# Writing down VectorE's order in an expert stream, with gathered rows used one block later

## The chip, the cores and the metric

One core of a Trainium2 chip runs the whole program. The metric is the device time of one execution in microseconds (us); the median of three runs of the kernel before is 4095.1 us (4092.52 to 4101.62). The engines are TensorE (PE in the profile; PEld is its weight load), VectorE (DVE), ScalarE (ACT), GpSimd (POOL) and SyncE (SP, which here only issues transfers).

## The reference

Two transformer blocks run one after the other on 512 tokens of width 1024. Each ends in a layer of 16384 single-row experts, which is the part that matters here:

```python
def block(xb):                                  # 128 tokens
    q = (xb @ w_q).reshape(PEER_BLOCK, PEER_HEADS, 2, PEER_QDIM // 2)
    s = jnp.einsum('thsd,hsnd->thsn', q, sub_keys)
    sv, si = lax.top_k(s, PEER_TOPK)            # 16 of 128 keys, twice, for 8 heads
    ...
    e = jnp.take_along_axis(cidx, pos, axis=-1) # 128 experts for each token
    g = jax.nn.softmax(top, axis=-1)
    act = jax.nn.gelu(jnp.einsum('thkd,td->thk', u_tab[e], xb), approximate=False)
    w = (g * act).astype(xb.dtype)
    return jnp.einsum('thk,thkd->td', w, v_tab[e])
```

Everything is float32. The kernel splits a float32 operand into a high half (rounded to TensorE's fp32r) and a low half (the rest), and takes three products: high by high, low by high, high by low.

## The kernel before

The program has two expert streams, one for each block of the network: about 960 to 1960 us and 3105 to 4085 us of the profile. Both are made by the function `peer`. Of the 512 tokens, 384 (three tiles) are *dense*: all 16384 experts are computed for them, 128 at a time, with gates that are zero where an expert was not picked. The fourth tile is *gathered*: for each of its 128 tokens the 128 picked rows of both tables are fetched by indirect transfers.

The stream's loop runs over e = 0 to 127, blocks of 128 experts. The names below are those of the profile.

- **A(e)**, `emit_A`, runs NA = 28 blocks ahead: `ur` is loaded (SP), `uh` is its high half (ScalarE), `ul` its low half (GpSimd, L1105), 24 products give `pa` (TensorE, L1112 to L1115), and ScalarE makes `ga`, the gelu of it.
- **Block e itself**: `vr` is loaded, `vh` is its high half (ScalarE, L1262), `vl` its low half (L1263; VectorE, but in the first stream GpSimd for e = 100 to 119). `w` is gate times `ga` (VectorE, L1267), `wh` and `wl` its halves (ScalarE L1268, VectorE L1269). 18 products, y(e), add them up over all 128 blocks (TensorE, L1293 to L1295). The tiles w, wh, wl, vh and vl have two buffers each, so wh(e), wl(e), vh(e) and vl(e) can be written only when y(e-2) has been read.
- **Gathered rows**: 128 events of kind u (`urow`: fetch the row k of every token, L1229; multiply by the token's input and sum into `act[:, k]`, L1230) and 128 of kind v (`vrow`: fetch, L1241; add `act` times the row to `acc`, L1243). After each 16 u there is a gelu on ScalarE (L1233) and a product with the gates on VectorE (L1234). The list `ev` has u alone first, then u and v in turn, then v alone; it is spread over blocks 2 to 100, some 2.6 rows in a block. The tiles `urow` and `vrow` have three buffers each.

Two things set the order. On TensorE, VectorE, ScalarE and SP, a planner that runs when the program is built takes the instruction that comes first in the program among those whose inputs it reckons ready. On GpSimd, within `manual_schedule`, the order is that of the program. After that each engine executes its own list strictly in order. In the list that the planner made for VectorE, w is two blocks ahead of its use, and the row instructions stand between vl, wl and w.

In the first stream a side job, `modulation` (L823, L825), runs on VectorE from e = 100.

Of the kernel before, what the change touches and what calls it, by code (L numbers as in the profile page):

```python
# [8 lines left out]
F32 = mybir.dt.float32  # L9
# [4 lines left out]
AF = mybir.ActivationFunctionType  # L14
OP = mybir.AluOpType
# [8 lines left out]
def build(tc, I, out, dbg=None, stop=None):  # L24
# [28 lines left out]
    def rsqrt(ssq, n, scale, nm, eps=EPS):  # L53
        """1 / sqrt(ssq * scale + eps) for a [128, n] tile."""
# [24 lines left out]
    def transpose_split(src, ncol, hi, lo, dst, psum=None):  # L79
        """src [128, ncol*128] -> hi/lo[:, k, dst] for each 128-column chunk k."""  # L80
        for k0 in range(0, ncol, 4):
            n = min(4, ncol - k0)
            pool, tag = psum or (pst, "tr")
            pt = pool.tile([128, 4, 128], F32, name="pt", tag=tag)
            for k in range(n):
                T.transpose(pt[:, k, :], src[:, (k0 + k) * 128:(k0 + k + 1) * 128], ident)
            split(dst_view(pt[:, 0:n, :], dst, src=True), dst_view(hi[:, k0:k0 + n, :], dst), dst_view(lo[:, k0:k0 + n, :], dst))
# [6 lines left out]
    def ssq_of(src, junk, nm):  # L94
        """sum of squares along the free axis on the scalar engine"""
        s = sm.tile([src.shape[0], 1], F32, name=nm, tag="ssq")
        A.activation(out=junk, in_=src, func=AF.Square, accum_out=s)
        return s
# [6 lines left out]
    def load_w(W, k, c0, cn, pool=None, e=V):  # L105
        """rows of chunk k of a weight matrix, as high and low halves"""
# [23 lines left out]
    def proj(hiT, loT, W, K, c0, cn, evac, tiles=range(NT), pool=None):  # L130
        """token-major product: for each token tile, psum[128, cn] = h @ W[:, c0:c0+cn]"""
# [16 lines left out]
    def keep_w(pool, W, K, c0, cn=512, last=0, e=V):  # L148
        """a block of weight columns on chip, for products of one token tile after the other"""
        room = [pool.tile([128, 2, 512], F32R, name=f"wk{i}") for i in range(K)]  # L150
        return [load_w(W, k, c0, cn, room[(k + K - last) % K], e) for k in range(K)]
# [10 lines left out]
    def proj_rows(hiT, loT, ws, evac, then):  # L162
        """all token tiles in turn; then(t) follows two tiles behind"""
# [7 lines left out]
    # token order of everything after the first mixing: row p of tile r is token 4 p + r  # L171
# [6 lines left out]
    # =====================================================================  # L178
    # block 1: norm, input projection
    # =====================================================================  # L180
# [43 lines left out]
    def head_proj(pool, hi, lo, W, c0, nh, hd, tiles, finish, first=None, wait=False):  # L224
        """nh heads of width hd divided by their root mean square; finish(t, heads, scale)"""
# [92 lines left out]
    def cmul(o_r, o_i, a_r, a_i, b_r, b_i, pool, shape, conj_b=False, e=V):  # L318
        """o = a * b (or a * conj b)"""
# [22 lines left out]
    # powers a^0 .. a^8  # L342
# [14 lines left out]
    # c a^n: real part and negated imaginary part  # L357
# [16 lines left out]
    # unit phases e^{i Theta j}, Theta = 8 theta, and the decay of a chunk  # L374
# [37 lines left out]
    def coefficients():  # L412
        s5x = ExitStack()
        s5t = s5x.enter_context(tc.tile_pool(name="s5t", bufs=1, side="right"))
        # chunk-input coefficients, transposed to [(s, c), pair, (g2, p)]
# [12 lines left out]
        # block-Toeplitz matrices [(s, c_in), g, (t, c_out)], two groups of a pair at a time  # L428
# [94 lines left out]
    def norm_T(xt, gain, hi, lo, sl, pool, inplace=False, two=False):  # L523
        """rmsnorm of a [128, 1024] tile with gain, transposed and split"""
# [218 lines left out]
    def softmax_row(ps, n, z, pool, tag="pe"):  # L743
        """exp(scores - max) with its sum"""
# [43 lines left out]
    def modulation(rows, pool, psum, tags, ptag, on_pool):  # L788
        """rows of the modulation; yields after each block of 128 x 1024 weights"""
# [57 lines left out]
    EV = 100  # L847
# [6 lines left out]
    def queries(qp, Wq, hi, lo):  # L854
        """loads, halves and products of the 128-column blocks of the query weights"""
# [31 lines left out]
    def peer_route(rw, query, keysT, crep, E, GT, ahead, also, first):  # L887
        """expert indices (as float) and gates, [128, tile, 128 slots]

        Step l of 16 is one half of one head's query; the candidates of a head are  # L890
        looked up in the steps of the next head, and products of the first expert
        blocks run between the steps' products."""
# [23 lines left out]
        def top16(src, work, vals, idx, tiles):  # L916
            """the 16 largest of src[:, t] with their places, in order"""
# [96 lines left out]
        def more(e):  # L1014
            """product e, then the halves of block e + 2, whose room it frees"""
# [39 lines left out]
    RG = (3, 6, 9, 11)  # L1055

    def peer_front(nm, Wq):
        """room for the transposed input, and for its making"""
# [11 lines left out]
    def peer(keysT_d, U, UT, Vt, front, finish, nm, side=None, also=None, then=None):  # L1070
# [86 lines left out]
        # slot-major indices and gates of the dense tokens  # L1157
        # first index = 16 a + b; rows a, b, second index (bf16 holds them) and gate
# [68 lines left out]
        def g_u(k):  # L1227
            row = gw.tile([128, 1024], F32, name="urow", tag="row")
            G.indirect_dma_start(out=row, out_offset=None, in_=U, in_offset=bass.IndirectOffsetOnAxis(ap=ei[:, TL, k:k + 1], axis=0))  # L1229
            V.scalar_tensor_tensor(out=row, in0=row, scalar=1.0, in1=hg_, op0=OP.mult, op1=OP.mult, accum_out=act[:, k:k + 1])  # L1230

        def g_w(k0):
            A.activation(out=act[:, k0:k0 + 16], in_=act[:, k0:k0 + 16], func=AF.Gelu)  # L1233
            V.tensor_tensor(out=act[:, k0:k0 + 16], in0=act[:, k0:k0 + 16], in1=GT[:, TL, k0:k0 + 16], op=OP.mult)  # L1234

        vrow = {}

        def g_v(k):
            if k < 128:
                vrow[k] = gw.tile([128, 1024], F32, name="vrow", tag="vrow")  # L1240
                G.indirect_dma_start(out=vrow[k], out_offset=None, in_=Vt, in_offset=bass.IndirectOffsetOnAxis(ap=ei[:, TL, k:k + 1], axis=0))  # L1241
            if k >= 2:
                V.scalar_tensor_tensor(out=acc, in0=vrow.pop(k - 2), scalar=act[:, k - 2:k - 1], in1=acc, op0=OP.mult, op1=OP.add)  # L1243

        ev = []
        for k in range(128 + 34):
            if k < 128:
                ev.append((g_u, k))
                if k % 16 == 15:
                    ev.append((g_w, k - 15))  # L1250
            if k >= 32:
                ev.append((g_v, k - 32))

        pend = []
        for e in range(128):
# [6 lines left out]
            A.copy(out=vh, in_=vr)  # L1262
            (G if side and EV <= e < EW else V).tensor_tensor(out=vl, in0=vr, in1=vh.bitcast(F32), op=OP.subtract)  # L1263
# [3 lines left out]
            V.tensor_tensor(out=w.rearrange("p (a b) -> p a b", b=TG), in0=gbuf[:, :, e % EB, :], in1=gas.pop(e).rearrange("p (a b) -> p a b", b=TG), op=OP.mult)  # L1267
            A.copy(out=wh, in_=w)  # L1268
            V.tensor_tensor(out=wl, in0=w, in1=wh.bitcast(F32), op=OP.subtract)  # L1269
            with tc.manual_schedule(engines={mybir.EngineType.Pool}):  # L1270
                if e + NA < 128:
                    emit_A(e + NA)
                want = min(len(ev), max(0, (len(ev) * (e + 1 - GS) + GE - 1) // GE))
                while nev < want:
                    f_, k_ = ev[nev]
                    f_(k_)
                    nev += 1
# [47 lines left out]
    def fin1(t, acc, pool, psum):  # L1325
        """sum, then the first normalization of the second block"""
# [30 lines left out]
    def first_rows():  # L1357
        """the second block's first projection, by token tiles"""
# [12 lines left out]
    # lambda of the differential attention, on every partition  # L1371
# [48 lines left out]
    # =====================================================================  # L1420
    # block 2
    # =====================================================================
# [23 lines left out]
    def rope_proj(which, dst, c0, nh, col, first=None):  # L1446
        """projection, head norm, rotation and transposition of nh heads, from 128-column chunk c0 of dst on"""
# [77 lines left out]
    # the residual waits in memory while its room holds the values  # L1525
# [52 lines left out]
    def projT(hi, lo, W, K, c0, evac, n=4):  # L1578
        """feature-major product: for each 128-column chunk, psum[128, tokens] = W[:, chunk].T @ h"""
# [190 lines left out]
def sincos(nc, pool, ang, shape, c, s):  # L1770
    """cosine and sine of any angle: reduced by whole turns in three exact steps"""
# [20 lines left out]
def host_arrays(a):  # L1792
    """layout only"""
# [73 lines left out]
```

## Time and profile before

| | |
|---|---|
| median of three runs | 4095.1 us (4092.52 to 4101.62) |
| profiled execution, first to last instruction | 4090.4 us |
| TensorE busy (weight load) | 3876.8 us, 95% (3370.2 us, 82%) |
| VectorE busy | 3004.6 us, 73% |
| ScalarE busy | 1654.8 us, 40% |
| GpSimd busy | 2145.8 us, 52% |
| bytes moved | 784.31 MB, mean 192 GB/s |
| mean granted TensorE clock | 0.975 of full speed |

The profile is of one execution, whose own time is known only as its span of 4090.4 us; what lies outside the first and the last instruction is the 4.7 us to the median. An engine's busy time leaves out its waits, which the views below put down to what ended them. A matmul's end is modelled, so starts of matmuls are the safe figures.

### The profile page before, as it was taken

Reading aid. Unit: us, or ns where it says so; the run is one execution under the profiler, and the core shown is the slowest. Engines: PE = TensorE matmul, PEld = TensorE weight load, DVE = VectorE, ACT = ScalarE, POOL = GpSimd, SP = SyncE. Lnnn points to the kernel's source line nnn. Section 1 sums busy time; section 2 is a strip of 40 time slices with the busy share of each in tenths; the row PEclk is TensorE's granted clock in tenths of the full one; section 3 lists DMA queues with packets and bytes.
Section 4 is the critical chain, followed back from the end, with each engine's and each line's share of the span. In section 5 each row is a group of like instructions: output and inputs, shape, how many; then the busy total and the mean of one; then the engine's idle time right before and its main releaser. Section 6 shows DMA issues by size and latency. Waiting matters only on the chain. (4 is left out here: it accounts for less than half of the span.)

```text
span 4090.4 us, 53234 instructions
## 1 busy us (share of the span) xinstructions
PE 3876.8 (95%) x19062; PEld 3370.2 (82%) x19062; DVE 3004.6 (73%) x5440; ACT 1654.8 (40%) x2567; POOL 2145.8 (52%) x1353
## 2 busy tenths in 40 slices
PE   6999998899999999989899988999899999999999
PEld 5777788899899999877777766788899899989887
DVE  8456489884787778777756566689884788878765
ACT  3454432454333333323444567332454333333333
POOL 3000057655777777754424433257655777776740
PEclk8999999999999999999999989999999999999999
DMA  3333132236898889986222323332237898888874
GB/s 112 99 111 106 52 113 79 101 134 230 302 319 320 315 311 315 318 275 221 90 81 57 93 75 100 102 114 79 98 134 250 299 322 314 311 306 308 299 254 150
DMA packets 330057, 784.31 MB, mean 192 GB/s; under 512 B 32048, under 2 KB 148864, under 8 KB 326400
## 3 DMA queue, kind: packets, MB, share of 16 engines
q1 hardware_dynamic: 252608, 499.86, 36.4%
q0 software_dynamic: 77184, 281.05, 19.5%
q8 instruction: 150, 2.46, 0.2%
q14 instruction: 115, 0.94, 0.1%
HBM read 722.98 MB, written 56.65 MB: 191 GB/s over the span
## 5 line engine op out<-in xcount | busy, mean ns | idle before, releaser
L1105 POOL TENSOR_TENSOR ul<-ur,uh 128x1024 fp32r<-128x1024 f32 x256 | 676.5, 2643 | 378.0 <-ACT uh L1099 259.5
L1112 PE MATMUL pa<-phi,uh 128*128 128x384 f32 x2048 | 695.5, 340 | 0.8 <-ACT ga L1117 0.8
L1113 PE MATMUL pa<-plo,uh 128*128 128x384 f32 x2048 | 694.8, 339 | 0.0
L1294 PE MATMUL y<-vl,wh 128*128 128x512 f32 x1536 | 606.2, 395 | 26.1 <-DVE vl L1263 22.4
L1295 PE MATMUL y<-vh,wl 128*128 128x512 f32 x1536 | 609.2, 397 | 11.3 <-DVE wl L1269 11.3
L1293 PE MATMUL y<-vh,wh 128*128 128x512 f32 x1536 | 603.8, 394 | 1.3 <-ACT wh L1268 1.2
L1243 DVE SCALAR_TENSOR_TENSOR acc<-vrow,act,acc 128x1024 f32<-128x1024 f32 x256 | 392.3, 1532 | 196.6 <-DMA vrow<-in_expert_v_dram,ei 99.5
L1230 DVE SCALAR_TENSOR_TENSOR urow<-urow,hgat 128x1024 f32<-128x1024 f32 x256 | 392.0, 1534 | 172.0 <-DMA urow<-in_peer_u_dram,ei 85.5
L1268 ACT CAST wh<-w 128x384 fp32r<-128x384 f32 x256 | 131.2, 513 | 736.0 <-PE y L1294 483.8
L1099 ACT CAST uh<-ur 128x1024 fp32r<-128x1024 f32 x256 | 269.3, 1052 | 382.9 <-PE pa L1113 149.2
L1115 PE MATMUL pa<-phi,ul 128*128 128x384 f32 x2048 | 402.5, 339 | 18.0 <-POOL ul L1105 17.9
L1112 PEld LDWEIGHTS pa<-phi,uh 128*128 128x128 f32 x2048 | 389.0, 190 | 10.0 <-ACT ga L1117 1.1
L1113 PEld LDWEIGHTS pa<-plo,uh 128*128 128x128 f32 x2048 | 389.1, 190 | 9.6
L1263 DVE TENSOR_TENSOR vl<-vr,vh 128x1024 fp32r<-128x1024 f32 x236 | 353.4, 1498 | 34.6 <-DMA ur<-in_peer_uT_dram 16.2
L1115 PEld LDWEIGHTS pa<-phi,ul 128*128 128x128 f32 x2048 | 362.0, 190 | 19.9 <-POOL ul L1105 19.9
L1206 PE MATMUL pgg<-oh,oh 128*128 128x128 f32 x1536 | 374.3, 421 | 4.4 <-DVE oh L1198 3.9
L1206 PEld LDWEIGHTS pgg<-oh,oh 128*128 128x128 f32 x1536 | 369.9, 337 | 7.1 <-issue 5.3
L1294 PEld LDWEIGHTS y<-vl,wh 128*128 128x128 f32 x1536 | 290.5, 189 | 93.5 <-DVE vl L1263 32.3
L1295 PEld LDWEIGHTS y<-vh,wl 128*128 128x128 f32 x1536 | 290.5, 189 | 85.0 <-DVE wl L1269 22.5
L1293 PEld LDWEIGHTS y<-vh,wh 128*128 128x128 f32 x1536 | 290.8, 189 | 55.5 <-ACT wh L1268 1.7
L77 DVE TENSOR_TENSOR wl<-wr,wh 128x512 fp32r<-128x512 f32 (+1 forms) x276 | 198.9, 729 | 148.9 <-ACT wh L76 148.8
L1200 POOL TENSOR_TENSOR oh<-oha,ohb 128x1024 f32<-128x1024 f32 x72 | 218.2, 3033 | 143.9 <-PE pgg L1206 104.5
(539 smaller groups left out, 7694.7 us busy)
## 6 DMA issues: line engine op xcount, KB each, us to landing
vr<-in_peer_v_dram SPq DMA_DIRECT2D x128, 512.0 KB
ur<-in_peer_uT_dram SPq DMA_DIRECT2D x128, 512.0 KB
vr<-in_expert_v_dram SPq DMA_DIRECT2D x128, 512.0 KB
ur<-in_expert_uT_dram SPq DMA_DIRECT2D x128, 512.0 KB
gbuf<-Gd SPq DMA_DIRECT2D x64, 768.0 KB
Gd<-stg SPq DMA_DIRECT2D x24, 1920.0 KB
wr<-in_w_in_dram SPq DMA_DIRECT2D x104, 256.0 KB
war<-in_w_ada_dram SPq DMA_DIRECT2D x24, 512.0 KB
```

The costliest lines, as they stand in the source:

```text
L1099: A.copy(out=uh, in_=ua[e])
L1105: G.tensor_tensor(out=ul, in0=raw, in1=uh.bitcast(F32), op=OP.subtract)
L1112: T.matmul(pa, uh[:, k, :], hi[:, k, 0:NDT], start=(k == 0), stop=False)
L1113: T.matmul(pa, uh[:, k, :], lo[:, k, 0:NDT], start=False, stop=False)
L1115: T.matmul(pa, ul[:, k, :], hi[:, k, 0:NDT], start=False, stop=(k == 7))
L1206: T.matmul(pg[:, j, :], oh2[:, :, 4 * q + j], oh1[:, :, 4 * q + j], start=True, stop=True)
L1230: V.scalar_tensor_tensor(out=row, in0=row, scalar=1.0, in1=hg_, op0=OP.mult, op1=OP.mult, accum_out=act[:, k:k + 1])
L1243: V.scalar_tensor_tensor(out=acc, in0=vrow.pop(k - 2), scalar=act[:, k - 2:k - 1], in1=acc, op0=OP.mult, op1=OP.add)
L1263: (G if side and EV <= e < EW else V).tensor_tensor(out=vl, in0=vr, in1=vh.bitcast(F32), op=OP.subtract)
L1293: T.matmul(y[t][c], wh[:, ts], vh[:, cs_], start=(e_ == 0), stop=False)
L1294: T.matmul(y[t][c], wh[:, ts], vl[:, cs_], start=False, stop=False)
L1295: T.matmul(y[t][c], wl[:, ts], vh[:, cs_], start=False, stop=(e_ == 127))
```

## The change

In the stream's loop, VectorE joins GpSimd under `manual_schedule`: its instructions there are executed in the order of the text. The text is put in this order: w, (wh, vh on ScalarE), vl, wl, then A(e+28), then the uses of the rows that were fetched in the block before, and last the fetches of the next rows. `g_u` and `g_v` are split into a fetch and a use. The gelu and the gate product follow the use of each 16th u at once. The v rows were used two fetches after their own; now all rows are used one block after it. The event list holds 256 entries instead of 266. In the first stream, vl of e = 100 to 119 on GpSimd now stands in the ordered part too, ahead of that block's fetches.

```diff
-        def g_u(k):
-            row = gw.tile(...)                       # fetch and use in one event
-            G.indirect_dma_start(out=row, ...)
-            V.scalar_tensor_tensor(out=row, in0=row, ..., accum_out=act[:, k:k + 1])
-        def g_v(k):
-            ...                                      # fetch row k, use row k - 2
+        def u_in(k):
+            rows_[0, k] = gw.tile([128, 1024], F32, name="urow", tag="row")
+            G.indirect_dma_start(out=rows_[0, k], ...)
+        def u_use(k):
+            row = rows_.pop((0, k))
+            V.scalar_tensor_tensor(out=row, in0=row, scalar=1.0, in1=hg_, ..., accum_out=act[:, k:k + 1])
+            if k % 16 == 15:
+                k0 = k - 15
+                A.activation(out=act[:, k0:k0 + 16], in_=act[:, k0:k0 + 16], func=AF.Gelu)
+                V.tensor_tensor(out=act[:, k0:k0 + 16], ..., in1=GT[:, TL, k0:k0 + 16], op=OP.mult)
+        def v_in(k): ...                             # fetch
+        def v_use(k): ...                            # acc += act[k] * row
...
-            A.copy(out=vh, in_=vr)
-            (G if side and EV <= e < EW else V).tensor_tensor(out=vl, in0=vr, in1=vh.bitcast(F32), op=OP.subtract)
...
-            V.tensor_tensor(out=w..., in0=gbuf[:, :, e % EB, :], in1=gas.pop(e)..., op=OP.mult)
-            A.copy(out=wh, in_=w)
-            V.tensor_tensor(out=wl, in0=w, in1=wh.bitcast(F32), op=OP.subtract)
-            with tc.manual_schedule(engines={mybir.EngineType.Pool}):
+            with tc.manual_schedule(engines={mybir.EngineType.Pool, DVE_}):
+                V.tensor_tensor(out=w..., in0=gbuf[:, :, e % EB, :], in1=gas.pop(e)..., op=OP.mult)
+                A.copy(out=wh, in_=w)
+                A.copy(out=vh, in_=vr)
+                (G if side and EV <= e < EW else V).tensor_tensor(out=vl, in0=vr, in1=vh.bitcast(F32), op=OP.subtract)
+                V.tensor_tensor(out=wl, in0=w, in1=wh.bitcast(F32), op=OP.subtract)
                 if e + NA < 128:
                     emit_A(e + NA)
+                for _, use, k in due:
+                    use(k)
                 want = min(len(ev), max(0, (len(ev) * (e + 1 - GS) + GE - 1) // GE))
-                while nev < want:
-                    f_, k_ = ev[nev]
-                    f_(k_)
-                    nev += 1
+                due = ev[nev:want]
+                nev = want
+                for get, _, k in due:
+                    get(k)
```

## Rows read from the trace of the kernel before

**Rows 1.** Stretches: us, length, busy us (instructions) by engine, clock, DMA share, GB/s.
```profile
983.00:1107.00 124.00, 118.75 (x588) 104.89 (x588) 89.24 (x114) 42.56 (x60) 84.27 (x51) 1.00 0.82 292
1107.00:1680.00 573.00, 573.00 (x2903) 521.56 (x2902) 468.52 (x484) 206.81 (x281) 431.49 (x251) 1.00 0.89 317
...
1807.00:1960.00 153.00, 134.54 (x581) 107.29 (x580) 117.56 (x130) 48.35 (x72) 58.40 (x24) 0.94 0.67 214
```

**Rows 2.** Timeline of TensorE: a y between two A; y(1), y(99) of both streams, one late y.
```profile
3339.15 0.40 PE L1293 MATMUL y<-vh,wh 128*128 128x512 f32 x1
...
3343.28 0.34 PE L1112 MATMUL pa<-phi,uh 128*128 128x384 f32 x1
...
3347.44 0.40 PE L1293 MATMUL y<-vh,wh 128*128 128x512 f32 x1
...
979.16 0.39 PE L1293 MATMUL y<-vh,wh 128*128 128x512 f32 x1
...
1806.89 0.39 PE L1293 MATMUL y<-vh,wh 128*128 128x512 f32 x1
...
3124.96 0.40 PE L1293 MATMUL y<-vh,wh 128*128 128x512 f32 x1
...
3587.95 0.39 PE L1293 MATMUL y<-vh,wh 128*128 128x512 f32 x1
...
3597.10 0.34 PE L1112 MATMUL pa<-phi,uh 128*128 128x384 f32 x1
...
3957.93 0.40 PE L1293 MATMUL y<-vh,wh 128*128 128x512 f32 x1
```

**Rows 3.** TensorE's waits (total, times, longest us): first stream, then second.
```profile
PE y L1294 <- DVE vl L1263: 10.3, 9, 2.5
PE y L1295 <- DVE wl L1269: 9.2, 4, 5.7
...
PE y L1294 <- DVE vl L1263: 12.1, 11, 2.9
PE y L1295 <- DVE wl L1269: 2.1, 1, 2.1
```

**Rows 4.** Timeline of VectorE, where v rows alone are fetched.
```profile
1734.62 1.29 DVE L1243 SCALAR_TENSOR_TENSOR acc<-vrow,act,acc 128x1024 f32<-128x1024 f32 x1 [3.35 <-DMA vrow<-in_peer_v_dram,ei]
```

**Rows 5.** VectorE's groups, 1107 to 1680 us (busy, mean ns, idle before, releaser).
```profile
L1230 DVE SCALAR_TENSOR_TENSOR urow<-urow,hgat 128x1024 f32<-128x1024 f32 x91 | 147.8, 1624 | 45.0 <-DMA urow<-in_peer_u_dram,ei 44.6
L1243 DVE SCALAR_TENSOR_TENSOR acc<-vrow,act,acc 128x1024 f32<-128x1024 f32 x90 | 140.6, 1562 | 60.0 <-DMA vrow<-in_peer_v_dram,ei 59.7
L1263 DVE TENSOR_TENSOR vl<-vr,vh 128x1024 fp32r<-128x1024 f32 x69 | 106.1, 1538 | 0.0
```

**Rows 6.** Timeline of VectorE in the middle of the first stream.
```profile
1405.98 1.21 DVE L1263 TENSOR_TENSOR vl<-vr,vh 128x1024 fp32r<-128x1024 f32 x1
1407.12 0.55 DVE L1269 TENSOR_TENSOR wl<-w,wh 128x384 fp32r<-128x384 f32 x1
1407.59 1.27 DVE L1243 SCALAR_TENSOR_TENSOR acc<-vrow,act,acc 128x1024 f32<-128x1024 f32 x1
1408.79 1.21 DVE L1230 SCALAR_TENSOR_TENSOR urow<-urow,hgat 128x1024 f32<-128x1024 f32 x1
...
1411.72 3.42 DVE L1263 TENSOR_TENSOR vl<-vr,vh 128x1024 fp32r<-128x1024 f32 x1
```

**Rows 7.** Timeline of GpSimd over the same us as Rows 6.
```profile
1410.68 3.37 POOL L1105 TENSOR_TENSOR ul<-ur,uh 128x1024 fp32r<-128x1024 f32 x1 [2.20 <-ACT uh L1099]
```

**Rows 8.** Timeline of VectorE and ScalarE at a w that came late.
```profile
1063.41 2.75 DVE L1267 TENSOR_TENSOR w<-gbuf,ga 128x384 f32<-128x384 f32 x1
...
1066.27 0.51 ACT L1268 CAST wh<-w 128x384 fp32r<-128x384 f32 x1 [6.48 <-DVE w L1267]
1066.69 1.05 ACT L1262 CAST vh<-vr 128x1024 fp32r<-128x1024 f32 x1
```

**Rows 9.** Timeline of GpSimd: a fetch that waited for a row's buffer.
```profile
1726.31 1.69 POOL L1241 DMA_INDIRECT vrow<-in_peer_v_dram,ei  x1 [1.36 <-DVE acc L1243]
```

More of the change, by code (lines that the diff above doesn't have):

```diff
@@ L1055, in build @@
     RG = (3, 6, 9, 11)
+    DVE_ = mybir.EngineType.DVE
     def peer_front(nm, Wq):
@@ L1225, in peer @@
         TL = ND
-        def g_u(k):
-            row = gw.tile([128, 1024], F32, name="urow", tag="row")
-            G.indirect_dma_start(out=row, out_offset=None, in_=U, in_offset=bass.IndirectOffsetOnAxis(ap=ei[:, TL, k:k + 1], axis=0))
-            V.scalar_tensor_tensor(out=row, in0=row, scalar=1.0, in1=hg_, op0=OP.mult, op1=OP.mult, accum_out=act[:, k:k + 1])
-        def g_w(k0):
-            A.activation(out=act[:, k0:k0 + 16], in_=act[:, k0:k0 + 16], func=AF.Gelu)
-            V.tensor_tensor(out=act[:, k0:k0 + 16], in0=act[:, k0:k0 + 16], in1=GT[:, TL, k0:k0 + 16], op=OP.mult)
@@ L1236, in peer @@
-        vrow = {}
-        def g_v(k):
-            if k < 128:
[L1240 to L1250, printed above, removed]
+        rows_ = {}
@@ new lines, in u_in @@
+        def u_in(k):
+            rows_[0, k] = gw.tile([128, 1024], F32, name="urow", tag="row")
+            G.indirect_dma_start(out=rows_[0, k], out_offset=None, in_=U, in_offset=bass.IndirectOffsetOnAxis(ap=ei[:, TL, k:k + 1], axis=0))
+        def u_use(k):
+            row = rows_.pop((0, k))
+            V.scalar_tensor_tensor(out=row, in0=row, scalar=1.0, in1=hg_, op0=OP.mult, op1=OP.mult, accum_out=act[:, k:k + 1])
+            if k % 16 == 15:
+                k0 = k - 15
+                A.activation(out=act[:, k0:k0 + 16], in_=act[:, k0:k0 + 16], func=AF.Gelu)
+                V.tensor_tensor(out=act[:, k0:k0 + 16], in0=act[:, k0:k0 + 16], in1=GT[:, TL, k0:k0 + 16], op=OP.mult)
@@ new lines, in v_in, with v_use @@
+        def v_in(k):
+            rows_[1, k] = gw.tile([128, 1024], F32, name="vrow", tag="vrow")
+            G.indirect_dma_start(out=rows_[1, k], out_offset=None, in_=Vt, in_offset=bass.IndirectOffsetOnAxis(ap=ei[:, TL, k:k + 1], axis=0))
+        def v_use(k):
+            V.scalar_tensor_tensor(out=acc, in0=rows_.pop((1, k)), scalar=act[:, k:k + 1], in1=acc, op0=OP.mult, op1=OP.add)
+        ev = []
+        for k in range(128 + 32):
+            if k < 128:
+                ev.append((u_in, u_use, k))
@@ L1251, in peer @@
             if k >= 32:
-                ev.append((g_v, k - 32))
+                ev.append((v_in, v_use, k - 32))
+        due = []
         pend = []
@@ L1266, in peer @@
             wl = tb_.tile([128, NDT], F32R, name="wl", tag="wl")
-            V.tensor_tensor(out=w.rearrange("p (a b) -> p a b", b=TG), in0=gbuf[:, :, e % EB, :], in1=gas.pop(e).rearrange("p (a b) -> p a b", b=TG), op=OP.mult)
-            A.copy(out=wh, in_=w)
-            V.tensor_tensor(out=wl, in0=w, in1=wh.bitcast(F32), op=OP.subtract)
-            with tc.manual_schedule(engines={mybir.EngineType.Pool}):
+            with tc.manual_schedule(engines={mybir.EngineType.Pool, DVE_}):
+                V.tensor_tensor(out=w.rearrange("p (a b) -> p a b", b=TG), in0=gbuf[:, :, e % EB, :], in1=gas.pop(e).rearrange("p (a b) -> p a b", b=TG), op=OP.mult)
+                A.copy(out=wh, in_=w)
+                A.copy(out=vh, in_=vr)
+                V.tensor_tensor(out=vl, in0=vr, in1=vh.bitcast(F32), op=OP.subtract)
+                V.tensor_tensor(out=wl, in0=w, in1=wh.bitcast(F32), op=OP.subtract)
                 if e + NA < 128:
                     emit_A(e + NA)
+                for _, use, k in due:
+                    use(k)
                 want = min(len(ev), max(0, (len(ev) * (e + 1 - GS) + GE - 1) // GE))
-                while nev < want:
-                    f_, k_ = ev[nev]
-                    f_(k_)
-                    nev += 1
+                due = ev[nev:want]
+                nev = want
+                for get, _, k in due:
+                    get(k)
             if side and e >= EM:
```

## The prediction

> **What bounds the kernel now.** I read the stretches first [rows 1]. In the middle of the first expert stream TensorE is busy for all of 573.00 us at full clock, while VectorE has 468.5 us of work: there TensorE is the bound and no order on VectorE can give anything. In the 124 us ahead of it, where u rows alone are fetched, TensorE is busy for 118.75. So the change is worth what TensorE loses at the ends, and costs whatever it adds to VectorE in the middle.
>
> How much is lost comes from the starts of matmuls [rows 2]. In steady state y starts every 3347.44 - 3339.15 = 8.29 us: 4.13 for y and 4.16 for A. From y(1) to y(99) are 98 such steps, which is 812.4 us. The first stream took 1806.89 - 979.16 = 827.7, the second 3957.93 - 3124.96 = 833.0. The excess is 15.3 and 20.6, together 35.9 us. What TensorE waited for is VectorE: vl nine times and eleven times, wl four times and once [rows 3]. The waits in [rows 3] are shorter than the excess, since products that follow a gap start more slowly. Of the excess, 5.0 us is one late y in the middle of the second stream, which took 3597.10 - 3587.95 = 9.15 in place of 4.13; I put the rest, 30.9, down to the stretches where one kind of row alone is fetched, since the middle of the first stream has none.
>
> Why vl is late there: VectorE stands at a row that has not landed, for 3.35 us in one case [rows 4], and vl is behind it in the list. In the middle VectorE also waits for rows, 44.6 + 59.7 us over 69 blocks, 1.51 us in a block [rows 5]; with 468.5 / 69 = 6.79 us of work that fills the 8.29, and vl never waits for anything else (idle 0.0). TensorE is not held up by that, because vl is far enough ahead: it may run from the end of y(e-2), plus 1.6 us for wh and vh and 1.2 for itself, and is needed A + y + A = 12.5 us after that end. VectorE may thus fall behind by 9.7 us before TensorE stands.
>
> **Part by part.**
>
> *Work on VectorE* is neither added nor removed: 256 row instructions, one w, vl and wl to a block, in both versions. Undisturbed, they issue 1.14 us (vl), 0.47 (wl) and 1.20 (a row) after one another [rows 6]; w has the shape of wl, 0.47. With 256/99 = 2.59 rows a block this is 1.14 + 0.94 + 2.59 x 1.19 = 5.2 us. Measured is 6.79. The missing 1.6 us is GpSimd's low half of u, which shuts VectorE out: one vl took 3.42 instead of 1.21 us while ul ran on GpSimd [rows 6, 7], a loss of 2.2 us, and there is one ul to a block.
>
> *Rows used one block later.* A row fetched in block e is now used behind vl and wl of block e+1. In the middle, where u and v take turns and three buffers of each hold more than two blocks' rows, it has landed by then, and the 1.51 us of waits in a block go. Where one kind is alone, its 2.59 rows a block go through three buffers: a fetch waits for the use that frees its buffer, and the row lands late. A fetch that began at 1726.31 [rows 9] is the one used at 1734.62 [rows 4], three uses behind the one that freed its buffer: 8.3 us. With the use and the hand-over (1.28 + 1.36) a buffer takes some 11 us to come round, and three rows in 8.29 x 3 / 2.59 = 9.6 us are wanted. So in these 12 or so blocks at either end the waits do not go; but they now stand behind the block's vl and wl, and what is late next is the w of the next block. That is 1.4 us too much a round, 1.2 us a block; 12 blocks put VectorE 14 us behind, of which 9.7 are free. The rest, 4.3 us in each of four stretches, is 17 us that would stay; nothing is the other bound. I take 10.3, a third of the 30.9, as both streams' first stretch begins with VectorE ahead, and let the 5.0 in the middle go.
>
> *w moves from two blocks ahead to right ahead of vl.* This is the cost. ScalarE makes wh, then vh, and vl needs vh. A w that was late shows the price: it ended at 1066.16, wh followed at 1066.27, vh ended at 1067.74 [rows 8], so 1.6 us from w to vl. If ScalarE's list has vh(e) ahead of wh(e) wherever w comes last, the price is nothing; if wh is always first, as in those rows, it is 1.6 us of idle VectorE a block. Which it is, the trace of before cannot show, since the planner makes ScalarE's list anew. The bounds of VectorE's block are so 6.8 and 8.4 us. I take half, 7.6, since w now ends near the moment that y(e-2) ends, and either can be first. At 7.6 us it stays hidden under TensorE's 8.29; at 8.4 it falls behind 0.1 us a block, 11 us in 98, and the 9.7 us still cover nearly all.
>
> *The gate product right behind the 16th u.* VectorE now waits for ScalarE's gelu eight times in a stream. Bounds are nothing and 6.5 us each, the longest that ScalarE stands in these rows [rows 8]. I take 0.5, as ScalarE is mostly idle; it comes out of the same 9.7 us.
>
> *vl of e = 100 to 119 under GpSimd's order* (first stream): the three fetches of e = 100 now stand behind vl(100), which needs vh. Those rows, their use and so the w of e = 102 come later by that vl; bounds are nothing and 3 us (a low half on GpSimd took 3.37 with VectorE in its way [rows 7]). Queued behind are VectorE's w and wl, and the side job. I take nothing. The stretch from y(99) on, with 18.5 us of idle TensorE and a granted clock of 0.94 [rows 1], is the side job's and I leave it as it is.
>
> *SP's queue* gets no new order, and the fetches are the same in number and size; 256 entries in place of 266 move none by more than a block.
>
> **Sum.** 30.9 x 2/3 + 5.0 = 25.6 us gained, nothing lost: 4090.4 - 25.6 = 4064.8 us of span. The profiled span lies 4.7 us below the median of the runs, so 4095.1 - 25.6 = 4069.5, say 4070 us.
>
> **Rivals.**
>
> *VectorE's block becomes the bound (slower).* The place is every block from 2 to 100, the mechanism the round trip w, wh, vh, vl together with ul. If wh is always first and ul hits in every block, the block is 5.2 + 1.6 + 2.2 = 9.0 us. It can hit in every block: if ScalarE takes uh right behind vh, ul asks just as VectorE runs vl and wl, and does not fall into the idle 1.6 us. From y(1) to y(99) that is 98 x 9.0 - 9.7 = 872 us, in place of 827.7 and 833.0: 83 us more, 4178. It decides from 8.57 us a block, (830.4 + 9.7) / 98, where 830.4 is the mean of the two streams now; between 8.57 and 9.0 lies everything from no change to +83, and late rows at the ends may add some 10 more. For it speak the rows of the late w, in which wh is first; against it, that today only 1.6 of 2.2 us are lost to ul, with VectorE hardly less busy.
>
> The Trainium skill, "SBUF — State Buffer", section "Who interferes with whom", says that a VectorE instruction with two inputs in SBUF and a GpSimd instruction that reads SBUF shut each other out for the whole instruction, in order of issue. The 3.42 us agree. By that rule each ul that meets a busy VectorE costs it all of ul's time, which is this rival's 2.2 us in every block, and 4178 us.
>
> *Nothing changes.* The rows that are fetched alone pass through three buffers no faster than before, whatever the order, and what TensorE loses at the ends is lost to that. From 30.9 / 4 + 9.7 = 17.4 us of delay in 12 blocks on, which is a round of 11.3 us in place of the 11, all 30.9 us stay and only the 5.0 go: 4090, less what the gate product takes. For it speaks the fetch that waited for the use [rows 9]; against it, that the one fetch shown need not be the typical one.
>
> *The order does not do what it says:* the gain in full, 35.9 us, 4059, if the rows at the ends land sooner once nothing stands in the way of their use. It is the lower end of the forecast's own range.
>
> **How the numbers follow.** The forecast (4058 to 4084) gets 0.43, the slower rival 0.38, no change (4087 to 4103) 0.17, anything else 0.02. About 8 us, 0.2%, is what a measurement of this kernel can tell from no change. The slower rival is nearly as likely as the forecast, so the range has to reach into it: from 4050, a little more than the full gain, to 4185, the rival at 9.0 us a block with some late rows. That leaves out less than 2 in 10. The likeliest case's own range is 4058 to 4084. Faster 0.44, same 0.17, slower 0.39.
>
> **What would show it.** Right: y starts every 8.29 us through both streams; VectorE's waits for rows in the middle go and vl waits for vh instead; VectorE's own chain is under 8.3 us. The price of moving w: idle time before vl, released by vh, near 0.8 us a block. Wrong: a step of y near 9 us in the middle stretch, TensorE waiting there for wl or vl in every block, wl or a row at 2.7 to 3.4 us in each block, just behind vl. No change: waits for rows before L1230 and L1243 at the ends as long as now, and TensorE waiting there for vl.

## The result and the profile after

| | before | after |
|---|---|---|
| median of 4 runs, us | 4093.8 (4080.0 to 4101.6) | 4036.3 (4029.1 to 4039.3) |
| ratio after / before, 95% interval | | 0.987 (0.9844 to 0.9896) |
| profiled execution, first to last instruction, us | 4090.4 | 4037.5 |

The change gained more than twice the 25.6 us of the forecast, and the time lies 14 us below the range. The profiles differ by 52.9 us.

**Two things about the change were read wrongly ahead of the run**, and all that follows should be read with them in mind. First, the diff printed above has one wrong line: the new line for vl is `V.tensor_tensor(out=vl, ...)` for every block. The condition `G if side and EV <= e < EW else V` is gone, and with it GpSimd's vl for e = 100 to 119 of the first stream; the sentence above on these vl "on GpSimd" is wrong in the same way. The change thus has a part of its own that was not costed: twenty vl move from GpSimd to VectorE. Second, the written order holds only among the instructions of one block. Blocks are not ordered against each other, and VectorE executes w(e+1) ahead of vl(e), in the changed kernel as in the one before. This comes from counting: each stream has 128 w and 128 vl on its engines, in the order of the blocks, and for every e from 2 to 98 of both streams the last w that starts ahead of vl(e) is w(e+1), in both kernels. So w was one block ahead of its use before, not two, and it is one block ahead still: it does not stand right ahead of its own vl.

Where the 52.9 us came from is counted by the starts of y, as in the prediction; y(k) is the y of block e = k. TensorE's timeline of the changed kernel at y(1) and y(99) of both streams [rows 2]:

```profile
979.38 0.39 PE L1299 MATMUL y<-vh,wh 128*128 128x512 f32 x1
...
1796.39 0.39 PE L1299 MATMUL y<-vh,wh 128*128 128x512 f32 x1
...
3095.54 0.40 PE L1299 MATMUL y<-vh,wh 128*128 128x512 f32 x1
...
3908.29 0.40 PE L1299 MATMUL y<-vh,wh 128*128 128x512 f32 x1
```

The same two stretches for all the kernels run, in us; "end" is the modelled end of the stream's last y:

| kernel | stream 1, y(1) to y(99) | y(99) to end | stream 2, y(1) to y(99) | y(99) to end |
|---|---|---|---|---|
| before | 827.7 | 153.6 | 833.0 | 123.6 |
| after | 817.0 | 137.1 | 812.8 | 120.6 |
| after, profiled again | 817.3 | 133.6 | 812.8 | 118.9 |
| vl of 100 to 119 on GpSimd | 818.4 | 150.0 | 812.8 | 118.8 |
| before, that vl on VectorE | 826.2 | 138.2 | 831.0 | 124.1 |
| VectorE's order left free | 823.1 | 140.6 | 818.4 | 125.4 |
| rows used in the same block | 816.4 | 138.2 | 817.5 | 123.8 |
| w right ahead of vl | 877.4 | 143.8 | 878.5 | 127.1 |
| the same, vh ahead of wh | 812.7 | 140.2 | 812.7 | 119.0 |
| three rows a block | 836.2 | 127.3 | 823.4 | 118.8 |

Of the 52.9 us, 10.7 + 20.2 = 30.9 come from y(1) to y(99), 16.5 from the first stream behind y(99), 3.0 from the second stream behind y(99), and 2.5 from the rest of the program. 98 undisturbed steps are 812.4 us: nothing is lost in the second stream any more, and 4.6 in the first.

The stretches of the changed kernel [rows 1] show the same: behind y(99) TensorE is busy for 131.39 of 137 us at a granted clock of 0.98, where it was 134.54 of 153 at 0.94, and GpSimd now does almost nothing there.

```profile
983.00:1107.00 124.00, 122.78 (x616) 110.04 (x615) 96.23 (x109) 44.21 (x63) 81.74 (x51) 1.00 0.87 297
1107.00:1680.00 573.00, 572.06 (x2896) 520.57 (x2897) 517.90 (x490) 208.63 (x282) 462.77 (x250) 1.00 0.91 317
...
1796.00:1933.00 137.00, 131.39 (x584) 105.51 (x583) 105.46 (x153) 49.47 (x73) 5.76 (x5) 0.98 0.74 246
```

VectorE's groups of the changed kernel from 1107 to 1680 us (busy, mean ns, idle before them, releaser) stand against [rows 5]. The 104.3 us of waits for rows are 0.7 now, and vl waits for vh instead, 54.3 / 69 = 0.79 us a block:

```profile
L1237 DVE SCALAR_TENSOR_TENSOR urow<-urow,hgat 128x1024 f32<-128x1024 f32 x91 | 153.1, 1682 | 0.0
L1248 DVE SCALAR_TENSOR_TENSOR acc<-vrow,act,acc 128x1024 f32<-128x1024 f32 x91 | 151.9, 1669 | 0.8 <-DMA vrow<-in_peer_v_dram,ei 0.7
L1273 DVE TENSOR_TENSOR vl<-vr,vh 128x1024 fp32r<-128x1024 f32 x71 | 97.7, 1377 | 54.3 <-ACT vh L1272 54.3
L1270 DVE TENSOR_TENSOR w<-gbuf,ga 128x384 f32<-128x384 f32 x70 | 91.3, 1304 | 0.0
```

The idle time is no loss: VectorE has caught up and waits until ScalarE may write the next wh, which is when y of two blocks earlier has let go of it. ScalarE's and VectorE's timelines of the changed kernel show it; wh starts at 1419.04, ahead of the w that starts at 1419.55, so it reads a w of the pass before:

```profile
1419.04 0.52 ACT L1271 CAST wh<-w 128x384 fp32r<-128x384 f32 x1 [3.45 <-PE y L1300]
1419.46 1.05 ACT L1272 CAST vh<-vr 128x1024 fp32r<-128x1024 f32 x1
...
1419.55 0.55 DVE L1270 TENSOR_TENSOR w<-gbuf,ga 128x384 f32<-128x384 f32 x1
1420.54 1.22 DVE L1273 TENSOR_TENSOR vl<-vr,vh 128x1024 fp32r<-128x1024 f32 x1 [0.44 <-ACT vh L1272]
```

### The profile page after: what moved, and what is told of

Same layout as the page of the kernel before. It is cut to its first block, busy times and chain, and to the rows that moved or that the text cites. A ratio compares the mean times of both kernels' runs of the same rounds, so it can differ in the third digit from the quotient of the medians.

```text
span 4037.5 us, 53263 instructions
## 1 busy us (share of the span) xinstructions
PE 3859.8 (96%) x19062; PEld 3367.6 (83%) x19062; DVE 3101.3 (77%) x5460; ACT 1659.2 (41%) x2567; POOL 2146.8 (53%) x1333
## 3 DMA queue, kind: packets, MB, share of 16 engines
q0 software_dynamic: 77184, 281.05, 19.5%
## 5 line engine op out<-in xcount | busy, mean ns | idle before, releaser
L1106 POOL TENSOR_TENSOR ul<-ur,uh 128x1024 fp32r<-128x1024 f32 x256 | 713.7, 2788 | 263.9 <-ACT uh L1100 177.1
L1299 PE MATMUL y<-vh,wh 128*128 128x512 f32 x1536 | 595.6, 392 | 1.7 <-ACT vh L1272 1.6
L1273 DVE TENSOR_TENSOR vl<-vr,vh 128x1024 fp32r<-128x1024 f32 x256 | 341.4, 1334 | 216.1 <-ACT vh L1272 215.9
L1248 DVE SCALAR_TENSOR_TENSOR acc<-vrow,act,acc 128x1024 f32<-128x1024 f32 x256 | 423.6, 1655 | 50.0 <-DMA vrow<-in_expert_v_dram,ei 25.3
L1237 DVE SCALAR_TENSOR_TENSOR urow<-urow,hgat 128x1024 f32<-128x1024 f32 x256 | 416.5, 1634 | 28.9 <-DMA urow<-in_peer_u_dram,ei 17.4
L1270 DVE TENSOR_TENSOR w<-gbuf,ga 128x384 f32<-128x384 f32 x256 | 261.8, 1024 | 45.7 <-DMA ur<-in_expert_uT_dram 21.6
```

The source lines that it names most:

```text
L1106: G.tensor_tensor(out=ul, in0=raw, in1=uh.bitcast(F32), op=OP.subtract)
L1248: V.scalar_tensor_tensor(out=acc, in0=rows_.pop((1, k)), scalar=act[:, k:k + 1], in1=acc, op0=OP.mult, op1=OP.add)
L1273: V.tensor_tensor(out=vl, in0=vr, in1=vh.bitcast(F32), op=OP.subtract)
L1299: T.matmul(y[t][c], wh[:, ts], vh[:, cs_], start=(e_ == 0), stop=False)
```

## The experiments

Ratios are to the kernel before on the same chip, whose median was 4081.0 us beside the first four kernels and 4086 beside the others. The changed kernel's own ratio is 0.987; a second measurement of it, beside the fifth and sixth kernel, shows how well it repeats.

> The changed kernel as it is, beside the others on the same chip: 4036 us, y(1) to y(99) at 817 and 813 us as in its first profile, if the profile of it that was read is a typical one. If the chip's executions differ by more than the stages compared, y(1) to y(99) move by several us too.

Measured: 0.9868 (0.9835 to 0.9901), 4025.7 us. The stretches between y(1) and y(99) repeat to 0.3 us; the 10 us to the first measurement lie outside them. So the stretches say more than the totals about what an edit did.

**The twenty vl.** In the changed kernel they go back to GpSimd; in the kernel before, with nothing else changed, they go to VectorE.

```diff
-                V.tensor_tensor(out=vl, ...)
+                (G if side and EV <= e < EW else V).tensor_tensor(out=vl, ...)
```

> The changed kernel (4036.3 us) with one line as it was: vl of e = 100 to 119 of the first stream is made on GpSimd again. Theory A, the engine of these twenty vl is what shortened the first stream behind y(99) (153.5 us before, 136.9 after): that stretch goes back to about 153, the time to about 4053. Theory B, the written order alone did it, as rows and side job no longer stand ahead of wl: the stretch stays within 3 us of 136.9, the time at 4036. The rest of both streams stays as it is by either.

> The kernel before (4093.8 us) with one line changed: vl of e = 100 to 119 of the first stream is made on VectorE, the order is left to the planner. Theory A, these twenty vl carry the gain behind y(99): 153.5 us there become about 137 and the time falls by some 16 us to about 4077. Theory B, without the written order the vl stands behind side job and rows on VectorE: nothing is gained or the stretch grows, 4094 or more. y(1) to y(99) stay at 827.7 and 833.0 by both.

Measured: back on GpSimd, 0.9919 (0.9894 to 0.9945), and 150.0 us behind y(99). In the kernel before on VectorE, 0.998 (0.9962 to 0.9998), and 138.2 us behind y(99) in place of 153.6. Theory A holds in both directions: of the 16.5 us the move of vl carries 13 to 15. The rest, 1 to 4 us, is no more than the 3.5 us by which two profiles of the changed kernel differ there, so no part of the written order is shown behind y(99). The time of the kernel before fell by 10 us with the move, where 16 were expected; single runs of either kernel spread over more than 20 us. Where the time goes shows in the groups of that stretch, first of the kernel before, then of the changed one:

```profile
L1295 PE MATMUL y<-vh,wl 128*128 128x512 f32 x173 | 70.8, 410 | 9.2 <-DVE wl L1269 9.2
...
L1263 POOL TENSOR_TENSOR vl<-vr,vh 128x1024 fp32r<-128x1024 f32 x20 | 55.6, 2778 | 61.0 <-ACT vh L1262 60.8
L825 DVE SCALAR_TENSOR_TENSOR am<-war,cc,am 128x1024 f32<-128x1024 f32 x21 | 34.4, 1640 | 6.8 <-DMA war<-in_w_ada_dram 6.6
...
L1269 DVE TENSOR_TENSOR wl<-w,wh 128x384 fp32r<-128x384 f32 x29 | 31.0, 1068 | 14.4 <-ACT wh L1268 14.4
```

```profile
L1301 PE MATMUL y<-vh,wl 128*128 128x512 f32 x173 | 67.4, 400 | 0.0
...
L1273 DVE TENSOR_TENSOR vl<-vr,vh 128x1024 fp32r<-128x1024 f32 x27 | 33.0, 1221 | 19.6 <-ACT vh L1272 19.6
...
L825 DVE SCALAR_TENSOR_TENSOR am<-war,cc,am 128x1024 f32<-128x1024 f32 x21 | 26.8, 1278 | 0.1
L1274 DVE TENSOR_TENSOR wl<-w,wh 128x384 fp32r<-128x384 f32 x27 | 14.8, 550 | 0.0
```

On GpSimd a vl takes 2.78 us, on VectorE 1.22. While GpSimd held vl, VectorE's wl took 1.07 us in the mean instead of 0.55 and the side job's steps 1.64 instead of 1.28, and TensorE waited 9.2 us for wl. All of that went although VectorE got twenty instructions more: its busy time fell from 117.6 to 105.5 us.

**Order or lag.** One kernel keeps the later use of rows in the text and leaves VectorE's order to the planner; the other keeps the written order and puts the loop of fetches ahead of that of uses, so that rows are used in the block in which they are fetched.

```diff
-            with tc.manual_schedule(engines={mybir.EngineType.Pool, DVE_}):
+            with tc.manual_schedule(engines={mybir.EngineType.Pool}):
```

> The changed kernel with VectorE's order left to the planner; rows are still used in the text one block behind their fetch, GpSimd's order is written out as before. Theory A, the order (vl and wl ahead of rows) is what freed TensorE: the 10.7 and 19.8 us of y(1) to y(99) come back, about 4067 us. Theory B, the block of lag is what matters, as a row that has landed holds nobody up wherever it stands: 4036 to 4042.

> The changed kernel with its written order, but the rows are used in the block in which they are fetched, still behind vl and wl. Theory A, the order is what matters: VectorE's waits for rows come back (about 1.5 us a block in the middle, 8.3 us from fetch to landing at the ends) but stand behind vl and wl, and TensorE keeps its 8.29 us: 4036 to 4046. Theory B, the block of lag is what matters: the waits for rows push the next block's vl past y, and the 30 us of y(1) to y(99) come back, about 4067 us, or more where the wait now falls in every block.

Measured: order free 0.9923 (0.9895 to 0.9951), written order without the lag 0.9892 (0.9868 to 0.9916). Of the 30.9 us from y(1) to y(99) the order without the lag kept 26.8 (11.3 + 15.5). What the change holds besides the order, which is the lag in the text, the gate product behind its 16th u and the shorter list, kept 19.2 (4.6 + 14.6). Theory A holds for the order. It was wrong in expecting that nothing at all would be left without it; Theory B is wrong too, since the planner put the uses where they stop VectorE as before. VectorE's groups from 1107 to 1680 us, first with the order free, then with the order but no lag:

```profile
L1248 DVE SCALAR_TENSOR_TENSOR acc<-vrow,act,acc 128x1024 f32<-128x1024 f32 x90 | 145.4, 1616 | 58.7 <-DMA vrow<-in_peer_v_dram,ei 58.0
L1237 DVE SCALAR_TENSOR_TENSOR urow<-urow,hgat 128x1024 f32<-128x1024 f32 x89 | 124.3, 1396 | 44.6 <-DMA urow<-in_peer_u_dram,ei 44.2
L1273 DVE TENSOR_TENSOR vl<-vr,vh 128x1024 fp32r<-128x1024 f32 x69 | 117.2, 1699 | 0.0
```

```profile
L1237 DVE SCALAR_TENSOR_TENSOR urow<-urow,hgat 128x1024 f32<-128x1024 f32 x90 | 136.7, 1519 | 46.3 <-DMA urow<-in_peer_u_dram,ei 46.3
L1248 DVE SCALAR_TENSOR_TENSOR acc<-vrow,act,acc 128x1024 f32<-128x1024 f32 x91 | 136.7, 1502 | 49.0 <-DMA vrow<-in_peer_v_dram,ei 48.7
L1273 DVE TENSOR_TENSOR vl<-vr,vh 128x1024 fp32r<-128x1024 f32 x70 | 87.3, 1247 | 3.1 <-ACT vh L1272 2.9
```

Both wait for rows some 100 us here, as the kernel before did, and it costs TensorE next to nothing: y(14) to y(84) of the first stream took 581.7 us before, 582.4 with the order free and 581.9 without the lag, where 70 undisturbed steps are 580.3. (In the second stream the kernel before took 588.9 us, with late steps at y(56) and y(80), the other two 582.3 and 581.2.) So these waits for rows in the middle of the first stream, which the change removes so visibly, were worth little. The ends are another matter. These are VectorE's groups from y(1) to y(14) of the second stream, where u rows alone are fetched: the kernel before, the changed one, the order free, the order without the lag:

```profile
L1230 DVE SCALAR_TENSOR_TENSOR urow<-urow,hgat 128x1024 f32<-128x1024 f32 x33 | 48.2, 1469 | 37.8 <-DMA urow<-in_expert_u_dram,ei 37.8
...
L1237 DVE SCALAR_TENSOR_TENSOR urow<-urow,hgat 128x1024 f32<-128x1024 f32 x31 | 39.4, 1300 | 8.3 <-DMA urow<-in_expert_u_dram,ei 8.2
...
L1237 DVE SCALAR_TENSOR_TENSOR urow<-urow,hgat 128x1024 f32<-128x1024 f32 x33 | 50.8, 1549 | 37.0 <-DMA urow<-in_expert_u_dram,ei 36.9
...
L1237 DVE SCALAR_TENSOR_TENSOR urow<-urow,hgat 128x1024 f32<-128x1024 f32 x32 | 46.4, 1475 | 21.4 <-DMA urow<-in_expert_u_dram,ei 21.4
```

Over y(1) to y(14) and y(84) to y(99) of both streams VectorE stood before uses of rows for 149 us in the kernel before, 150 with the order free, 79 with the order but no lag and 68 in the changed kernel. So the written order does two things where TensorE loses: it takes vl and wl out from behind the rows, and it halves the waits for rows. How much of the 26.8 us either is worth was not separated. The waits are not all of it, since the free order waits as long as the kernel before and loses less. Which rows of the free order cost the first kernel its 11.7 us is not settled: the losses lie in the first 14 blocks (12.22 us for one step) and around y(95).

**w really ahead of its vl.** One written order over blocks 2 to 99, in place of one for each block, does what the prediction took the change to do. A second kernel has ScalarE's vh ahead of wh as well.

```diff
+            if e == 2:
+                whole = tc.manual_schedule(engines={mybir.EngineType.Pool, DVE_})
+                whole.__enter__()
...
+            if e == EM - 1:
+                whole.__exit__(None, None, None)
```

```diff
-                A.copy(out=wh, in_=w)
-                A.copy(out=vh, in_=vr)
+                with tc.manual_schedule(engines={mybir.EngineType.Activation}):
+                    A.copy(out=vh, in_=vr)
+                    A.copy(out=wh, in_=w)
```

> The changed kernel with one written order over blocks 2 to 99 in place of one for each block, so that w of a block really stands right ahead of its own vl (it stands one vl and wl earlier in the changed kernel). ScalarE still takes wh ahead of vh. Theory A, the slower rival of the prediction: w, wh, vh, vl is a round trip that costs VectorE 1.6 us in each block on top of 5.2 and of 2.2 for GpSimd's low half; y starts every 9.0 us, y(1) to y(99) take about 872 us in each stream, the time is about 4156. Theory B: GpSimd's low half falls into that wait, or the wait into VectorE's idle 0.8 us, and y stays at 8.29 us: 4036 to 4046.

> The same as the kernel with w right ahead of vl, and in addition ScalarE takes vh ahead of wh in every block. Theory A: the 1.6 us from w to vl are gone, since vh no longer stands behind w; VectorE's block is 7.4 us and y stays at 8.29 us, about 4036 to 4046, whatever the other kernel shows. Theory C, w right ahead of vl is slow for another reason (a later w delays wl, or holds its buffer): this kernel is as slow as the other one.

Measured: 1.0231 (1.0197 to 1.0265), 4174.0 us; with vh first 0.987 (0.9832 to 0.9907), 4024.6 us. Theory A holds for both: y(14) to y(84) took 634.65 / 70 = 9.07 us a block where 9.0 was expected. The time came out 18 us above the 4156 expected; 12 of them lie between y(1) and y(99). The timelines of VectorE and of GpSimd in the slow kernel show the round trip and the low half of u that falls on what follows:

```profile
1407.05 0.59 DVE L1273 TENSOR_TENSOR w<-gbuf,ga 128x384 f32<-128x384 f32 x1
1409.24 1.23 DVE L1276 TENSOR_TENSOR vl<-vr,vh 128x1024 fp32r<-128x1024 f32 x1 [1.60 <-ACT vh L1275]
1410.39 2.75 DVE L1277 TENSOR_TENSOR wl<-w,wh 128x384 fp32r<-128x384 f32 x1
...
1410.25 2.47 POOL L1106 TENSOR_TENSOR ul<-ur,uh 128x1024 fp32r<-128x1024 f32 x1 [2.26 <-ACT uh L1100]
```

This was no chance meeting: in 1107 to 1680 us all 63 wl of this kernel took 2.75 us in the mean, and 101.2 / 63 = 1.6 us of idle time stood before each vl:

```profile
L1277 DVE TENSOR_TENSOR wl<-w,wh 128x384 fp32r<-128x384 f32 x63 | 173.3, 2752 | 0.0
...
L1276 DVE TENSOR_TENSOR vl<-vr,vh 128x1024 fp32r<-128x1024 f32 x63 | 77.2, 1226 | 101.2 <-ACT vh L1275 101.2
```

With vh first no step from y(1) to y(99) of either stream is over 8.6 us, and the 4.6 us that the changed kernel still loses in its first stream are gone too. The measurement can't tell its total from the changed kernel's.

**How near the row buffers are to their limit.** `GE = 99` becomes `GE = 86`: the same rows in fewer blocks.

> The changed kernel with GE = 86 in place of 99: the same 256 rows in fewer blocks, 2.98 a block, so that where one kind of row is alone three rows are wanted in 8.29 x 3 / 2.98 = 8.35 us. Theory A: a row buffer comes round in 6.8 (median from issue to landing) + 1.28 + 1.36 = 9.4 us, which the changed kernel's 9.6 covered and 8.35 does not: 1.1 us a block over some 11 blocks is 12 us, of which 9.7 are free, so about 2 us are lost in each of four stretches: 4044, y(1) to y(14) some 2 us longer. Theory B, the 11 us of the prediction are the round and the changed kernel escaped by something else: 28 us behind in 11 blocks, 18 lost in each of four stretches, about 4110, y(1) to y(14) near 126. Theory C, the round does not matter, rows land whenever they are asked for: 4036, no step over 8.6 us in the second stream.

Measured: 0.9916 (0.9888 to 0.9945), 4049.0 us. Against the changed kernel y(1) to y(14) grew by 8.8 and 5.2 us and y(84) to y(99) by 12.7 and 5.5, while the middle stayed at 580.5. Theory C is out. The round of a buffer can be read from GpSimd's fetches, as the third fetch behind takes the same buffer: here from the 100th to the 128th v row of the first stream, 28 fetches.

```profile
1620.00 1.02 POOL L1245 DMA_INDIRECT vrow<-in_peer_v_dram,ei  x1 [1.10 <-DVE acc L1248]
...
1709.75 2.05 POOL L1245 DMA_INDIRECT vrow<-in_peer_v_dram,ei  x1 [1.36 <-DVE acc L1248]
```

That is 89.8 / 28 x 3 = 9.6 us for three fetches; the other three stretches give 9.3, 9.5 and 9.3, where 8.35 were wanted. So the round is near theory A's 9.4 and not theory B's 11. The loss is more than theory A's 2 us all the same, and it is not one mechanism: most of it falls in single steps. The step from y(9) to y(10) took 14.32 and 12.51 us in the two streams. There the loss came through GpSimd, where a fetch that waits for a buffer stands ahead of the next block's ul, and A waits for that. GpSimd's timeline of the first stream there, and TensorE's:

```profile
1054.85 1.81 POOL L1233 DMA_INDIRECT urow<-in_peer_u_dram,ei  x1 [5.50 <-DVE urow L1237]
1056.96 1.31 POOL L1233 DMA_INDIRECT urow<-in_peer_u_dram,ei  x1 [0.30 <-issue]
1058.28 2.36 POOL L1106 TENSOR_TENSOR ul<-ur,uh 128x1024 fp32r<-128x1024 f32 x1
...
1060.69 0.69 PE L1116 MATMUL pa<-phi,ul 128*128 128x384 f32 x1 [4.52 <-POOL ul L1106]
```

The step from y(88) to y(89) of the first stream took 19.52 us, 11.2 more than undisturbed, which is nearly all of that stretch's 12.7. There the side job stood ahead of vl on VectorE. Its tiles share the rows' buffers (tags `vrow` and `row`), and it starts just behind the last fetch, at 1710.9 us, in place of 1802.7 in the changed kernel:

```profile
1711.72 7.16 DVE L825 SCALAR_TENSOR_TENSOR am<-war,cc,am 128x1024 f32<-128x1024 f32 x2
1718.80 1.22 DVE L1273 TENSOR_TENSOR vl<-vr,vh 128x1024 fp32r<-128x1024 f32 x1
...
1720.07 0.80 PE L1300 MATMUL y<-vl,wh 128*128 128x512 f32 x1 [8.21 <-DVE vl L1273]
```

So the edit changed more than the rate of rows, and the 12.7 us do not measure the round.

## Why the prediction was wrong

*What failed first: the vl of e = 100 to 119, "I take nothing".* The step rested on a line of the diff that was misread, and it left the whole stretch from y(99) on "as it is". It was worth 13 to 15 us, shown by two kernels. The trace of before held the hint, and it was read wrongly as well: the four waits for wl in the first stream [rows 3], 9.2 us, were counted to the excess of y(1) to y(99). They all lie behind y(99), in the stretch with the clock of 0.94 [rows 1]; the 19.5 us of waits in the first stream would also be longer than its excess of 15.3, not shorter, as the prediction says of them. The kernel that the prediction costed, with these vl on GpSimd, is one of the experiments: its ratio of 0.9919 makes 4062 us out of 4095.1, an estimate inside the likeliest case's 4058 to 4084.

*What failed second: "a third stays".* 10.3 of the 30.9 us at the ends were to stay because a row buffer comes round in 11 us and 9.6 are wanted. That took one fetch that needed 8.3 us to land [rows 9] for the typical one. In the changed kernel the median where v is alone is 6.8 us (1680 to 1796, 32 fetches), a round of 6.8 + 1.28 + 1.36 = 9.4; with three rows a block 9.3 to 9.6 were measured. The trace of before could have told it, by the 28 fetches behind the 100th v row of its first stream:

```profile
1709.64 1.68 POOL L1241 DMA_INDIRECT vrow<-in_peer_v_dram,ei  x1 [1.60 <-DVE acc L1243]
...
1801.22 0.94 POOL L1241 DMA_INDIRECT vrow<-in_peer_v_dram,ei  x1 [0.30 <-issue]
```

That is 91.6 / 28 x 3 = 9.8 us for three; the four stretches give 9.6 to 10.1. In the changed kernel VectorE still waited for rows at the ends, 68 of 149 us, but it did not fall behind by the 9.7 us that are free: y(84) to y(99) took 124.4 us in both streams, 15 steps of 8.29. The gain from y(1) to y(99) was 30.9 in place of 25.6. That is about midway to the 35.9 of the rival with the full gain; what stayed, 4.6 us, lies in the first 17 blocks of the first stream.

*The step on w was wrong, and its sum right by accident.* w kept standing one vl and wl ahead of its own block, so the price of 0 to 1.6 us, of which 0.8 was taken, was never paid. The 0.79 us of idle time before vl, which the prediction named as its mark, is VectorE waiting for TensorE. The number matched and the reason did not.

*The slower rival was right on its condition.* Where w does stand right ahead of vl, y(1) to y(99) took 877 and 879 us; 872 was worked out. The Trainium skill, "SBUF — State Buffer", section "Who interferes with whom", says that a VectorE instruction with two inputs in SBUF and a GpSimd instruction that reads SBUF shut each other out for the whole instruction; the 2.75 us of wl, in place of 0.55, agree. What was wrong is the chance of 0.38: it hung on where w stands, which the order's text for one block does not settle.

*What held, and what did not quite.* TensorE bounds the middle. The 5.0 us of one late y there went: TensorE had waited 2.9 us in it, and its granted clock was 0.81 over those 9.2 us, 1.00 on either side. Of the 30.9 us that were put down to the ends, 2.8 stood at y(80) and y(84) of the second stream, where u and v still take turns; they went too. The waits for rows went in the middle, and at the ends they more than halved, where the prediction let them stay. The gate product behind the 16th u cost nothing: VectorE waited before none of its 16.

The sum again, in the profile's time: 25.6 forecast + 16.5 behind y(99) of the first stream + 5.3 more from y(1) to y(99) + 3.0 behind y(99) of the second + 2.5 elsewhere = 52.9. The 2.5 are within what two executions of the changed kernel differ by. The 3.0 are more than the 1.7 by which these two differ there, and neither the free order nor the order without the lag shows them; their cause stays open.

## What to carry to other kernels

Read the new line of each instruction that moves, engine included, before costing the order around it: here the engine of twenty instructions was worth a quarter of the gain. An order that is written for one pass of a loop says nothing about the next pass, so look in the list for which pass's instruction stands ahead; one place earlier or later for a small multiply was 60 us a stream here. A wait that fills an engine's idle time can be worth nothing: 104 us of them went from the middle of the first stream, and TensorE, which was busy throughout, gained nothing there.

## What the runs showed of the hardware that was not expected

Most of what two executions of the changed kernel differ by lies in a part that the change doesn't touch: the 1152 us between the streams took 1139 in the second profile, with TensorE busy for 1075.31 and 1065.16 us at the same granted clock of 0.96. In the ten profiles that part, from the last y of the first stream to the first of the second, took 1140 to 1156 us. What makes the difference there was not tried.

A low half on GpSimd can lock onto one VectorE instruction through the middle of a stream: with w right ahead of vl it met wl in every block from 1107 to 1680 us, since ScalarE's uh, which releases it, ended while vl ran in all 63, so that ul came in just ahead of wl. In the changed kernel the same ul spread over w (1304 ns in the mean, undisturbed 550) and the rows (1682 and 1669, undisturbed some 1220 and 1280), where VectorE had time for it.
